# One encoder layer on one core: the in-projection in two passes, with the neighbourhood attention by bands of eight rows inside the second

## The chip, the core and the metric

The kernel is one program on one core of a Trainium2 chip. TensorE (PE) does the matrix products, and its weight loads (PEld) run beside them. VectorE (DVE), ScalarE (ACT) and GpSimd (POOL) do the elementwise work. SyncE (SP) issues the DMAs, in the order of the program. Each engine runs its own list of instructions in order and waits at semaphores for the others. The metric is the device time of one execution, in microseconds (us).

## What is computed

Two sequences of vectors of 1024 numbers go through one encoder layer with the same weights: a prompt of 512 tokens (s=0 in the code) and a sample of 2048 (s=1). Tokens stand in a grid of 64 columns, so the prompt has 8 rows and the sample 32. Cut to what matters:

```python
x = layer_norm(x, emb_ln_g, emb_ln_b)
z = x @ w_in                                   # 1024 -> 1952
qa, ka, va, fb, cq, ckv, kr, sg = split(z, [256, 256, 256, 256, 256, 128, 32, 512])
o_a = natten(qa, ka, va, na_rpb)               # 4 heads of 64
o_b = real(fft2(fb))                           # Fourier mix
o_c = mla(cq, ckv, kr, ...)                    # 4 heads, every query to every key
o_d = gating(gelu(sg), ...)                    # tokens mixed in chunks of 128
x = layer_norm(ALPHA * x + concat(o_a, o_b, o_c, o_d) @ w_out, ...)
x = layer_norm(ALPHA * x + conv_ffn(x), ...)   # 1024 -> 5632 -> 1024

def natten(q, k, v, rpb):      # row r, column c of the grid
    r0, c0 = clip(r - 4, 0, rows - 8), clip(c - 8, 0, 64 - 16)
    s = q[r, c] . k[r0:r0+8, c0:c0+16] / 8 + rpb[head, row offset, column offset]
    return softmax(s over the 128 neighbours) @ v[r0:r0+8, c0:c0+16]
```

All of it is float32. A product of float32 matrices is made of three products of a narrower type: each operand is split into a high part (a cast) and a low part (the rest), and `mm3` adds high x high, high x low and low x high.

## The kernel before

**Stages.** In `build` the stages stand one behind another: `phase1` (layer norm, in-projection, gating), `fourier` (the Fourier mix) with `mla_prep` (queries, keys and values of MLA) stepped inside it at every second of its yields, `natten` (neighbourhood attention) with what is left of `mla_prep`, then `mla`, `outproj` and the feed-forward part. `mla` is a generator; `natten` calls its first step, `next(ahead)`, twelve units before its own end.

**Order on the engines.** A scheduler places the instructions in each engine's list when the program is built. The code's order and the buffers of the pools (a tile waits until the buffer that it reuses is free) bind it, so an instruction can stand somewhat ahead of or behind its place in the code.

**phase1** goes over five blocks of 512 tokens, block 0 the prompt. All 14 weight tiles are loaded and split at the start (`load_w`, the high part on ScalarE, the low part L132 on GpSimd, or from the sixth tile on in turns on VectorE and GpSimd). For a block, `norm` loads four x tiles, normalises them on VectorE (L153, L162), applies the affine of the layer norm on GpSimd (L166, L167) and stores them; `turn` transposes them on TensorE (L350) and splits the result into the operands xTh and xTl. A block then takes 13 features (f, 128 outputs by 512 tokens, 24 products L139 to L141 each, ending on ScalarE at L364 or, for gelu, L368), the token products (L380 to L382, 288 columns each), and the gating (L409 and what goes before it). The norm of block b+1 stands behind feature 2, its turn behind the token products. `sgu_consts` loads the matrix of the gating and transposes it (L278) at the start, ahead of the features.

**natten** runs with whole sequences: for each sequence and pair of heads the query and key of all rows are loaded and split. A *unit* is eight rows of queries (a band) by 16 columns by one head, 128 queries on partitions. Its neighbours lie in a window of up to 16 rows by 32 columns, so the score product is 128 x 512 at most. For a unit:

- scores: three products on TensorE (`mm3`, L139 to L141, tile s);
- L683 on VectorE adds the table of biases and masks and takes the extreme value, L686 on ScalarE is the exponential with its sum, then a reciprocal on VectorE, and L689 scales, on GpSimd (VectorE for the prompt);
- flip: up to four transposes on TensorE (L705), split in the evacuation into ph and pl;
- values: products L724 and L725, for a group of four bands together, into one bank of 512 columns (o) that a product with zeros clears first (L719). A chunk of keys serves one or two bands, so these are 128 or 256 columns wide.

There are 16 prompt and 64 sample units, the prompt first. The flip of a unit is put three units behind its scores, with three banks for scores and five E buffers. The value windows are transposed by L643 (80 times 128 x 128), the tables added up by L666.

## Time and profile before

| | us |
|---|---|
| median of 3 runs | 3288.79 (3282.6 to 3290.15) |
| the profiled execution | 3299.96 |
| its span in the trace | 3298.2 |
| TensorE busy in the span | 3152.9 (96%) |
| VectorE busy | 2130.4 (65%) |
| ScalarE busy | 1390.7 (42%) |
| GpSimd busy | 1617.3 (49%) |
| start and in-projection | 0 to about 490 |
| Fourier mix with the MLA preparation | about 490 to 640 |
| neighbourhood attention | about 640 to 855 |
| MLA, out-projection, feed-forward | from about 855 |

The granted clock is the share of full speed that the chip allowed TensorE, 0.962 as a mean over this execution; 1.00 stands for 2.4 GHz, 0.50 for 1.2 GHz, and a value between them is a stretch with both. A busy time of TensorE counts what its products last at the clock that they had. A matmul's own duration contains its way through the array, so the pace of a row of products is read from the distance of their starts. The borders between stages are soft: the last work of one lies beside the first of the next.

### The profile page before, as it was taken

Reading aid. Unit: us, or ns where it says so; the run is one execution under the profiler, and the core shown is the slowest. Engines: PE = TensorE matmul, PEld = TensorE weight load, DVE = VectorE, ACT = ScalarE, POOL = GpSimd, SP = SyncE. Lnnn points to the kernel's source line nnn. Section 1 sums busy time; section 2 is a strip of 40 time slices with the busy share of each in tenths; the row PEclk is TensorE's granted clock in tenths of the full one; section 3 lists DMA queues with packets and bytes.
Section 4 is the critical chain, followed back from the end, with each engine's and each line's share of the span. In section 5 each row is a group of like instructions: output and inputs, shape, how many; then the busy total and the mean of one; then the engine's idle time right before and its main releaser. Section 6 shows DMA issues by size and latency. Waiting matters only on the chain.

```text
span 3298.2 us, 45978 instructions
## 1 busy us (share of the span) xinstructions
PE 3152.9 (96%) x16119; PEld 2739.0 (83%) x16119; DVE 2130.4 (65%) x3770; ACT 1390.7 (42%) x2493; POOL 1617.3 (49%) x1329
## 2 busy tenths in 40 slices
PE   7899999889999999998999999999899999999997
PEld 6788888767789998886899989999799997877785
DVE  6322216666888887445788866665567557679668
ACT  3221225545777677223544444433344323234224
POOL 6322313336666565234888856541354215466446
PEclk9999999867999999998999999999899999999998
DMA  7222144533210011545676769996599877547652
GB/s 222 87 88 72 71 122 129 172 105 103 91 38 22 22 41 48 161 144 170 226 251 234 244 218 346 335 313 211 183 349 336 276 244 256 216 168 284 227 209 103
DMA packets 369156, 588.35 MB, mean 178 GB/s; under 512 B 48409, under 2 KB 246905, under 8 KB 367389
## 3 DMA queue, kind: packets, MB, share of 16 engines
q1 hardware_dynamic: 368924, 585.41, 52.0%
q8 instruction: 128, 2.10, 0.3%
q14 instruction: 104, 0.84, 0.1%
HBM read 393.80 MB, written 191.51 MB: 177 GB/s over the span
## 4 chain that ended last, share of the span: by engine, by line
PE 84%; DVE 6%; DMA 5%; ACT 2%; issue 2%; SPq 1%; POOL 1%; DVEq 0%; ACTq 0%; POOLq 0%
PE s L1257 6%; PE s L1258 6%; PE s L1259 6%; PE t L1452 6%; PE t L1257 5%; PE t L1258 5%; PE t L1259 5%; PE s L139 4%; PE s L1452 4%; PE s L140 4%; PE s L141 4%; PE o L1452 4%; PE t L954 3%; PE mm L141 3%; PE mm L140 3%; PE mm L139 3%
## 5 line engine op out<-in xcount | busy, mean ns | idle before, releaser
L132 POOL TENSOR_TENSOR w<-wraw,w 128x512 fp32r<-128x512 f32 x162 | 235.5, 1459 | 315.1 <-ACT w L122 269.4
L1258 PE MATMUL s<-B,w 128*128 128x450 f32 (+1 forms) x792 | 285.4, 360 | 6.4 <-DVE B L132 6.4
L1257 PE MATMUL s<-B,w 128*128 128x450 f32 (+1 forms) x792 | 285.7, 363 | 0.6 <-ACT B L122 0.6
L1259 PE MATMUL s<-B,w 128*128 128x450 f32 (+1 forms) x792 | 284.9, 360 | 0.0
L1258 PE MATMUL t<-T,w 128*128 128x450 f32 (+1 forms) x792 | 283.8, 358 | 0.0
L1259 PE MATMUL t<-T,w 128*128 128x450 f32 (+1 forms) x792 | 283.7, 358 | 0.0
L1257 PE MATMUL t<-T,w 128*128 128x450 f32 (+1 forms) x792 | 282.1, 360 | 0.9 <-ACT T L122 0.9
L1265 DVE SCALAR_TENSOR_TENSOR h<-h,convc,h 128x896 f32<-128x896 f32 (+1 forms) x132 | 215.2, 1661 | 0.0
L926 DVE TENSOR_SCALAR_CACHE_REDUCE a<-s,low 128x512 f32<-128x512 f32 x272 | 195.0, 745 | 30.6 <-PE t L954 24.5
L140 PE MATMUL mm<-xTl,a 128*128 128x512 f32 x520 | 206.6, 397 | 2.2 <-DVE xTl L132 2.2
L141 PE MATMUL mm<-xTh,a 128*128 128x512 f32 x520 | 202.8, 393 | 0.0
L1264 DVE SCALAR_TENSOR_TENSOR h<-h,convc,h 128x896 f32<-128x896 f32 (+1 forms) x132 | 168.9, 1310 | 50.7 <-ACT h L1263 50.7
L139 PE MATMUL mm<-xTh,a 128*128 128x512 f32 x520 | 198.5, 395 | 1.4 <-ACT xTh L122 0.7
L1452 PE MATMUL t<-w,go 128*128 128x512 f32 x696 | 195.0, 399 | 4.9 <-ACT go L122 1.8
L1263 ACT ACTIVATE h<-h,convc 128x896 f32<-128x896 f32 (+1 forms) x132 | 138.3, 1096 | 133.3 <-DVE h L1138 130.8
L132 DVE TENSOR_TENSOR a<-t,a 128x512 fp32r<-128x512 f32 x240 | 161.1, 682 | 35.3 <-ACT a L122 34.7
L122 ACT CAST w<-wraw 128x512 fp32r<-128x512 f32 x166 | 102.1, 618 | 191.9 <-PE t L1259 132.7
L122 ACT CAST a<-t 128x512 fp32r<-128x512 f32 x240 | 134.4, 585 | 78.4 <-PE t L954 76.1
L1452 PEld LDWEIGHTS t<-w,go 128*128 128x128 f32 x696 | 131.1, 189 | 39.5 <-DVE x L1319 4.0
L1258 PEld LDWEIGHTS s<-B,w 128*128 128x128 f32 x792 | 150.7, 190 | 15.4 <-DVE B L132 6.7
L954 PE MATMUL t<-ident,a 128*128 128x128 f32 x1088 | 156.3, 274 | 6.1 <-DVE a L132 4.3
L122 ACT CAST go<-gs 128x256 fp32r<-128x256 f32 x200 | 78.2, 405 | 196.8 <-PE t L1452 65.2
(365 smaller groups left out, 9184.6 us busy)
## 6 DMA issues: line engine op xcount, KB each, us to landing
w<-wuops SPq DMA_DIRECT2D x220, 512.0 KB
wuops<-w SPq DMA_DIRECT2D x110, 512.0 KB
w<-wdops SPq DMA_DIRECT2D x104, 512.0 KB
wraw<-in_w_up_dram SPq DMA_DIRECT2D x88, 512.0 KB
wdops<-xs SPq DMA_DIRECT2D x74, 512.0 KB
graw<-g SPq DMA_DIRECT2D x100, 256.0 KB
wd<-wdops SPq DMA_DIRECT2D x48, 512.0 KB
g<-h SPq DMA_DIRECT2D x44, 448.0 KB
```

The costliest lines, as they stand in the source:

```text
L122: nc.scalar.copy(out, src)
L132: e.tensor_tensor(lo, src, hi.bitcast(F32), op=ALU.subtract)
L139: mm(ps, wh, xh, start=first, stop=False)
L140: mm(ps, wh, xl, start=False, stop=False)
L141: mm(ps, wl, xh, start=False, stop=last)
L926: nc.vector.tensor_scalar(e[:, c * 512:c * 512 + 512], ps, 1.0, self.low, op0=ALU.mult, op1=ALU.max, accum_out=m4[:, c:c + 1])
L954: nc.tensor.transpose(pt[:, k], e[:, kk * P:(kk + 1) * P], self.ident)
L1257: mm(ps[:, :hw], a, xh[:, k, :hw], start=first and k == 0, stop=False, skip_group_check=True)
L1258: mm(ps[:, :hw], a, xl[:, k, :hw], start=False, stop=False, skip_group_check=True)
L1259: mm(ps[:, :hw], b, xh[:, k, :hw], start=False, stop=last and k == KH - 1, skip_group_check=True)
L1265: nc.vector.scalar_tensor_tensor(c[:, :n], hb[:, 2:n + 2], cw[:, 2, ft:ft + 1], c[:, :n], op0=ALU.mult, op1=ALU.add)
L1452: mm = lambda a, b, st, sp_: nc.tensor.matmul(ps, a, b, start=st, stop=sp_, skip_group_check=True)
```

## The change

**The in-projection goes over the blocks twice.** The *near* pass makes features 0 to 7 of every block (query, key and value of the attention, and the Fourier input). Only eight weight tiles are loaded ahead of it; the others, the gating's constants and those of the convolution are loaded in blocks 1 and 2. The norm of block b+1 stands behind feature 0 of block b. Features 6 and 7 go as a pair, and after each of their eight steps one operand of the next block is transposed and split. The operands are also kept: 80 stores of 256 KB into `xd` in DRAM. The *far* pass makes features 8 to 12, the token products and the gating, with the operands loaded again by 20 loads of 1 MB.

**The attention runs inside the far pass.** It is a generator; `spent` counts the columns of projection products and steps it each time a sum of 92 is reached (54 for six products of a feature, 64 for a part of the token products). It goes by bands, the sample first: each band loads and splits its own queries and keys (`band`), each window its own values (`window`), and a unit's values go into a bank of their own, all products 128 columns wide, without the product of zeros. Tables are 512 wide at most, scalings and tables are on GpSimd throughout, there are three E buffers, two banks for scores and two for transposes, one for values, and the flip stands two units behind the scores.

**What moves for it.** `mla_prep` is stepped in three of four yields of `fourier` and finished there. The first step of `mla` stands behind `fourier`. Of the list of instructions, PE's grows from 15961 to 16185, ACT's from 2299 to 2411, with 57 loads of a function table in place of 17.

```diff
+NEAR = 8
+BANDS = ((("P", 0, 8),), (("A", 0, 12), ("B", 4, 16), ("B", 12, 16), ("C", 20, 12)))
+TICK = 92
...
                     for i, _ in enumerate(self.fourier(w2, s2)):
-                        if i % 2 == 0:
+                        if i % 4 < 3:
                             next(prep, None)
+                    for _ in prep:
+                        pass
                 with tc.tile_pool(name="mls", bufs=2, reuse_waits="tile") as ms:
                     mla = self.mla(ms)
-                    for _ in self.natten(mla, mps, s1):
-                        next(prep, None)
+                    next(mla)
...
-                self.split(raw[:, :, :n], wh[f][:, :, c0:c0 + n], wl[f][:, :, c0:c0 + n], "act", "dve" if i > 4 and i % 2 else "pool")
+                self.split(raw[:, :, :n], wh[f][:, :, c0:c0 + n], wl[f][:, :, c0:c0 + n], "act", "dve" if i > 4 else "pool")
...
+                def keep(b, k):
+                    for i in range(2):
+                        self.store(self.xd[b][:, k, i], xT[b][k][i].bitcast(F32))
...
+                def turn(b, k):
+                    ps, x = operand(b, k)
+                    self.evac(ps, x[0], x[1])
+                    keep(b, k)
...
+                extra = [lambda i=i: load_w(i) for i in range(NEAR, len(src_off))] + [sgu_consts, conv_consts]
+                norm(0)
+                turn0()
+                for b in range(nb):
+                    for f in range(NEAR - 2):
...
+                        if f == 0 and b + 1 < nb:
+                            norm(b + 1)
...
+                        if b and f and extra:
+                            extra.pop(0)()
+                    pair = [self.t(pp, [P, 512], "mm", bufs=4) for _ in range(2)]
+                    for k in range(KD):
+                        for i in range(2):
+                            step(pair[i], b, NEAR - 2 + i, k)
+                        if b + 1 < nb:
+                            turn(b + 1, k)
...
+                def spent(n):
+                    acc[0] += n
+                    while acc[0] >= TICK:
+                        acc[0] -= TICK
+                        next(nat, None)
...
+                def feat(b, f, uT):
+                    ps = self.t(pp, [P, 512], "mm", bufs=3)
+                    for k in range(KD):
+                        x = X[b][k]
+                        self.mm3(ps, wh[f][:, k], wl[f][:, k], x[:, 0], x[:, 1], k == 0, k == KD - 1)
+                        if k % 2:
+                            spent(54)
...
+            ps = self.t(pp, [P, 512], "s", bufs=2)
...
+            e = self.t(wp, [P, 512], "E", bufs=3)
...
+            po = self.t(pp, [P, P], "o", bufs=1)
+            for k in range(nck):
+                v = vr[:, k, hh].rearrange("p a d -> p (a d)")
+                nc.tensor.matmul(po, v, p[:, 0, k], start=k == 0, stop=False)
+                nc.tensor.matmul(po, v, p[:, 1, k], start=False, stop=k == nck - 1)
...
+        N, LAG = len(units), 2
...
+        for x in range(N + LAG + 1):
+            at(values, x - LAG - 1)
+            at(flip, x - LAG)
+            if x < N:
+                u = units[x]
+                if u[4] == 0:
+                    window(*u[:4])
+                scores(u)
+                if x + 2 < N:
+                    table(*units[x + 2])
+                if u[3:] == (2, 0) and x + 4 < N:
+                    band(*units[x + 4][:3])
+            yield
```

In the listings of instructions below a row is a line of the kernel, the operation, output<-inputs by tile and number, the size. The changed kernel's lines are a few higher: L142 to L144 are its `mm3`, L729 is its flip, L741 and L742 its values, L684 its window transposes, L169 and L170 its affine. First, GpSimd at the start, before: the affine of block 1 (tiles x_494 to x_500; x_165 is block 0's last) and the low parts of weights (a_.._..<-uv).

```order
L167 TENSOR_TENSOR x_165<-x_165,eb_140 128x1024
L132 TENSOR_TENSOR a_61_149<-uv_348,a_61_149 128x1024
L166 TENSOR_TENSOR x_494<-x_494,eg_139 128x1024
L132 TENSOR_TENSOR a_63_151<-uv_356,a_63_151 128x1024
L167 TENSOR_TENSOR x_494<-x_494,eb_140 128x1024
L166 TENSOR_TENSOR x_496<-x_496,eg_139 128x1024
L167 TENSOR_TENSOR x_496<-x_496,eb_140 128x1024
L166 TENSOR_TENSOR x_498<-x_498,eg_139 128x1024
L132 TENSOR_TENSOR a_65_153<-uv_364,a_65_153 128x1024
L166 TENSOR_TENSOR x_500<-x_500,eg_139 128x1024
L167 TENSOR_TENSOR x_498<-x_498,eb_140 128x1024
L167 TENSOR_TENSOR x_500<-x_500,eb_140 128x1024
```

The same place of the changed kernel (block 1 is x_397 to x_403).

```order
L170 TENSOR_TENSOR x_170<-x_170,eb_163 128x1024
L169 TENSOR_TENSOR x_397<-x_397,eg_162 128x1024
L170 TENSOR_TENSOR x_397<-x_397,eb_163 128x1024
L169 TENSOR_TENSOR x_399<-x_399,eg_162 128x1024
L170 TENSOR_TENSOR x_399<-x_399,eb_163 128x1024
L169 TENSOR_TENSOR x_401<-x_401,eg_162 128x1024
L169 TENSOR_TENSOR x_403<-x_403,eg_162 128x1024
L170 TENSOR_TENSOR x_401<-x_401,eb_163 128x1024
L170 TENSOR_TENSOR x_403<-x_403,eb_163 128x1024
```

The weights' low parts have left the rows of block 1's affine. Second, TensorE in the attention, before, some way into the sample: scores (s), flips (t<-flip), values (o).

```order
L139 MATMUL s_6253<-a_993_5557,a_991_5555 128x512
L140 MATMUL s_6253<-a_994_5558,a_991_5555 128x512
L141 MATMUL s_6253<-a_993_5557,a_992_5556 128x512
L705 MATMUL t_6163<-flip_65,E_6076 128x128 x3
L725 MATMUL o_6181<-pl_6106,a_1064_5777 128x128
L139 MATMUL s_6272<-a_993_5557,a_991_5555 128x512
L140 MATMUL s_6272<-a_994_5558,a_991_5555 128x512
L141 MATMUL s_6272<-a_993_5557,a_992_5556 128x512
L724 MATMUL o_6181<-ph_6105,a_1064_5777 128x256
L725 MATMUL o_6181<-pl_6106,a_1064_5777 128x256
```

After, in the far pass (mm are features of the projection; s_3203 are the scores of the unit whose E is E_3207):

```order
L142 MATMUL s_3203<-a_585_2816,q_2813 128x512
L143 MATMUL s_3203<-a_585_2816,q_2813 128x512
L144 MATMUL s_3203<-a_585_2816,q_2813 128x512
L143 MATMUL mm_3406<-a_420_2182,a_66_148 128x512
L729 MATMUL t_3032<-flip_65,E_2934 128x128 x4
L684 MATMUL t_3043<-ident_60,vw_3040 128x128 x4
L144 MATMUL mm_3406<-a_420_2182,a_66_148 128x512
L142 MATMUL mm_3406<-a_420_2182,a_66_148 128x512
```

About a hundred rows later on TensorE, where that unit's flip stands, behind the values of an older one:

```order
L741 MATMUL o_3231<-p_3190,vt_3042 128x128
L742 MATMUL o_3231<-p_3190,vt_3042 128x128
L729 MATMUL t_3288<-flip_65,E_3207 128x128 x4
L684 MATMUL t_3299<-ident_60,vw_3296 128x128 x4
L142 MATMUL s_3449<-a_585_2816,q_2813 128x512
L143 MATMUL s_3449<-a_585_2816,q_2813 128x512
L144 MATMUL s_3449<-a_585_2816,q_2813 128x512
L142 MATMUL mm_3624<-a_598_2898,a_68_150 128x512
```

Projection products and the work of older units now stand between a unit's scores and its flip; the values are pairs of 128 columns. Third, SP where MLA begins, before: loads of MLA's key pieces (raw<-K, raw<-Kr) among those of the attention (a_888<-z, mask, tbl).

```order
L117 DMA V_44_117<-vp_5167 128x4x256
L114 DMA mask_5236<-in_na_mask_dram 128x256
L114 DMA a_888_5271<-z_3_18_91 128x512
L114 DMA tbl_5238<-R_118 128x1x256
L114 DMA tbl_5268<-R_118 128x1x256
L117 DMA Kr_42_115<-q_5226 32x512
L114 DMA a_888_5271<-z_5_20_93 128x512
L114 DMA raw_7154<-Kr_42_115 32x512
L114 DMA raw_7160<-K_40_113 64x512
L114 DMA raw_7160<-Kr_42_115 32x512
L114 DMA raw_7165<-K_40_113 64x512
L114 DMA raw_7165<-Kr_42_115 32x512
```

After (mix<-ob are the last stores of the Fourier mix):

```order
L120 DMA Kr_42_115<-q_8149 32x512
L120 DMA mix_36_109<-ob_8179 128x4x128
L120 DMA mix_36_109<-ob_8231 128x4x128
L120 DMA mix_36_109<-ob_8283 128x4x128
L120 DMA mix_36_109<-ob_8335 128x4x128
L117 DMA raw_8343<-K_40_113 64x512
L117 DMA raw_8343<-Kr_42_115 32x512
L117 DMA raw_8349<-K_40_113 64x512
L117 DMA raw_8349<-Kr_42_115 32x512
L117 DMA raw_8354<-K_40_113 64x512
L117 DMA raw_8354<-Kr_42_115 32x512
L117 DMA wraw_11006<-in_w_out_dram 128x1024
```

The loads of MLA's keys have moved from among the attention's to behind the Fourier mix, and a load of w_out stands among them.

## Rows read from the trace of the kernel before

**Rows 1.** Busy time by stretch: from:to, length, busy of each engine, clock, DMA, GB/s.
```profile
core 0: us, PE busy (x) PEld busy (x) DVE busy (x) ACT busy (x) POOL busy (x), PEclk, DMA share, GB/s
110.00:490.00 380.00, 377.19 (x2030) 321.37 (x2029) 102.35 (x291) 77.38 (x155) 88.64 (x41) 1.00 0.25 85
...
690.00:820.00 130.00, 121.61 (x534) 93.91 (x534) 82.42 (x221) 73.79 (x182) 68.41 (x71) 0.71 0.34 98
900.00:1200.00 300.00, 299.57 (x2044) 270.13 (x2042) 253.93 (x696) 218.51 (x332) 194.21 (x172) 1.00 0.11 30
```

**Rows 2.** L380 of two blocks: durations in ns, first to last start, form.
```profile
L380 PE MATMUL mm<-w,xTh x32: 288/294/297, 110.4 to 122.7; 128*128 128x288 f32 x32
...
L380 PE MATMUL mm<-w,xTh x32: 288/294/297, 201.3 to 213.6; 128*128 128x288 f32 x32
```

**Rows 3.** Three lines around the attention, in the same view.
```profile
L571 ACT COPY q<-t x5: 569/572/577, 521.0 to 648.4; 32x512 f32<-32x512 f32 x5
...
L926 DVE TENSOR_SCALAR_CACHE_REDUCE a<-s,low x272: 730/747/753, 854.7 to 1312.6; 128x512 f32<-128x512 f32 x136
...
L725 PE MATMUL o<-pl,a x160: 273/364/581, 646.4 to 864.7; 128*128 128x256 f32 x96, 128*128 128x128 f32 x64
```

**Rows 4.** L683 by stretch: length, VectorE busy (entries), clock, DMA, GB/s.
```profile
690.00:820.00 130.00, 31.75 (x94) 0.71 0.34 98
820.00:850.00 30.00, 9.56 (x28) 0.99 0.18 48
```

**Rows 5.** TensorE in order of time: start, us, line, operation, form.
```profile
200.38 0.39 PE L141 MATMUL mm<-xTh,a 128*128 128x512 f32 x1
200.60 0.39 PE L139 MATMUL mm<-xTh,a 128*128 128x512 f32 x1
...
842.30 0.36 PE L725 MATMUL o<-pl,a 128*128 128x256 f32 x1
842.50 0.28 PE L724 MATMUL o<-ph,a 128*128 128x256 f32 x1
842.62 0.28 PE L725 MATMUL o<-pl,a 128*128 128x256 f32 x1
...
1004.28 1.04 PE L954 MATMUL t<-ident,a 128*128 128x128 f32 x8
1005.08 0.36 PE L971 MATMUL o<-a,a 128*128 128x256 f32 x1
```

**Rows 6.** Five microseconds of the start, columns as in rows 1.
```profile
90.00:95.00 5.00, 0.00 (x0) 0.00 (x0) 1.67 (x1) 1.37 (x4) 4.29 (x2) 0.50 0.30 100
```

**Rows 7.** What TensorE waited for until 110 us: total, times, longest.
```profile
PE tr L278 <- DMA uv<-in_sgu_w_dram: 8.2, 1, 8.2
```

**Rows 8.** GpSimd in order of time, the affine of block 1.
```profile
63.34 2.39 POOL L166 TENSOR_TENSOR x<-x,eg 128x1024 f32<-128x1024 f32 x1 [4.63 <-DVE x L162]
...
81.04 2.84 POOL L132 TENSOR_TENSOR a<-uv,a 128x1024 fp32r<-128x1024 f32 x1
...
87.17 4.63 POOL L167 TENSOR_TENSOR x<-x,eb 128x1024 f32<-128x1024 f32 x2
```

**Rows 9.** Block 2's normalisation in order of time, SP, VectorE and GpSimd.
```profile
140.72 1.79 SPq L114 DMA_DIRECT2D x<-in_x_sample_dram  x4
...
L153 DVE BATCH_NORM_STATS2 ln0st<-x x8: 673/676/695, 144.0 to 151.2; 128x6 f32<-128x512 f32 x8
...
153.03 8.10 POOL L166 TENSOR_TENSOR x<-x,eg 128x1024 f32<-128x1024 f32 x3 [17.60 <-PE mm L141]
...
165.79 7.10 POOL L167 TENSOR_TENSOR x<-x,eb 128x1024 f32<-128x1024 f32 x3
```

**Rows 10.** A group of instructions by line: count, busy and mean ns, idle before.
```profile
L132 DVE TENSOR_TENSOR a<-raw,a 96x512 fp32r<-96x512 f32 x5 | 7.6, 1550 | 0.7 <-ACT a L122 0.7
```

**Rows 11.** ScalarE in order of time, a load of a function table.
```profile
127.20 1.28 ACT L146 ACT_TABLE_LOAD   x1
128.50 0.31 ACT L146 ACTIVATE sgls<-sgmv,eps_ln 128x16 f32<-128x16 f32 x1
```

More of the change, by code (lines that the diff above doesn't have):

```diff
@@ L205, in build @@
             self.g = d([NF, P, sum(T for _, T in SEQS)], "g")
+            self.xd = [d([P, KD, 2, 512], f"xd{b}") for b in range(5)]
             self.wu = d([NF, 5, P, D], "wuops")
@@ L416, in phase1 @@
[L416 to L448 removed]
+                    for k in range(KD):
+                        keep(0, k)
@@ new lines, in phase1, with z_out @@
+            self.blocks = blocks
+            with pool("p1x") as xp, pool("p1p", space=bass.MemoryType.PSUM) as pp:
+                near(xp, pp)
+            with pool("p1n") as wp2, pool("p1q", space=bass.MemoryType.PSUM) as pp:
+                far(wp2, pp)
+    def z_out(self, sp, b, f, ps):
+        s, t0 = self.blocks[b]
+        zs = self.t(sp, [P, 512], "zs", bufs=3)
+        self.nc.scalar.activation(zs, ps, AF.Copy, scale=-0.125 if f in (2, 3) else 1.0)
+        dst = self.z[s][f] if f < 8 else self.c[s][f - 8]
+        self.store(dst[:, t0:t0 + 512], zs)
@@ L647, in prologue_v @@
[L647 to L653 removed]
+            vp = self.t(wp, [P, 4, 2, 2, 64], "vt", bufs=2)
+            vr = vp.bitcast(F32R)
+            ps = self.t(pp, [P, 4, 2, 64], "t", bufs=2)
+            for k in range(nch):
+                nc.tensor.transpose(ps[:, k].rearrange("p h d -> p (h d)"), vc[:, k * P:(k + 1) * P], self.ident)
+            nc.scalar.copy(vr[:, :nch, :, 0], ps[:, :nch])
@@ L661, in table @@
-            for ty in sorted(set(C["types"])):
-                off, n, ro = NA_TYPES[ty]
-                a0 = h * RSZ + (RO + ro) * 32 - 8 * ct
-                self.load(tbl[:, off - lo_c:off - lo_c + n],
-                          bass.AP(self.R.tensor, self.R.offset + a0, [[32, 8], [1, 16], [1, n]]))
-            (nc.gpsimd if s else nc.vector).tensor_tensor(tbl, tbl, st["mask"], op=ALU.add)
-            st["tbl", s, h, ct] = tbl
+                last["mask"] = self.t(wp, [P, 512], "mask")
@@ L783, in natten_body @@
             yield
-        for p in pend:
-            values(*p[1])
-        st["cm"].__exit__(None, None, None)
     def fourier(self, wp, sp):
```

615 lines of the change are left out of this document (265 added, 350 removed).

## The prediction

> **What bounds the kernel now.** I read the table by stage first [rows 1]. The in-projection (until 490 us) keeps TensorE busy for 377 of 380 us at the full granted clock, and a block of 512 tokens takes 90.9 us, from one block's token products (L380) to the next one's [rows 2]. The stretch from 490 to 640 is the Fourier mix with the MLA preparation. The neighbourhood attention fills 640 to 855: in its largest part TensorE is shown busy for 122 of 130 us, but at a granted clock of 0.71, a mix of the levels 1.2 and 2.4 GHz. MLA behind it runs at 1.00. So the attention stage is the one place before MLA where TensorE's work is paid at a worse price than its size, and this is where the change can gain. The stage ends where MLA's first scores are reduced, at 854.7; its own last value product L725 starts at 864.7, so some 12 us of it already lie beside MLA [rows 3].
>
> What a unit (one band, 16 columns, one head) costs there: L683 runs once a unit and shows two entries for it, so 94 entries are 47 units in 130 us, 2.77 us each, at clock 0.71; and 28 are 14 units in 30 us, 2.14 us each, at 0.99 [rows 4]. At the full clock a product of 512 columns follows the last after 0.226 us (200.38 to 200.60), one of 256 after 0.12 (842.50 to 842.62), the first of another kind about 0.08 later than that (842.30 to 842.50), and eight of 128 take 0.80 (1004.28 to 1005.08) [rows 5].
>
> **The change, term by term, against the profiled run** (3299.96 us, span 3298.2; the median of the runs shown is 3288.79, 0.34% lower, and the result is scaled by that).
>
> 1. The stage of its own goes: 640 to 855, minus 215 us, and the 12 us of it that lie beside MLA's start: minus 12.
>
> 2. Its TensorE work returns inside the second pass. By columns: scores are 98,304 columns, 192 times 512, at 0.226 us: 43 us; 256 flips and 128 window transposes at 0.10: 38 us; 512 value products of 128 columns at 0.10: 51 us. That is 133 us. (Before, values were 192 products of 256 columns, 128 of 128 and 16 of zeros, and the window transposes 80: bands cost 16 us more.) A unit changes the kind of product four times: 80 x 4 x 0.08 = 26. Sum 159 us. Lower end 133; upper end the pace of [rows 4] at the full clock, 64 x 2.14 + 16 x 1.07 (prompt units, half the columns) + 16 = 170. I take 159: the 2.14 us still holds waits that projection products can fill here.
>
> 3. Waits of TensorE in the second pass: plus 5 us (0 to 25). In the order of instructions, priced by [rows 5], the flips of a sample unit stand 9 to 22 us of TensorE work behind its scores, its value products mostly 4 to 10 us behind the flips. Between lie a reduction, an exponential, a reciprocal and a scaling, then an evacuation. All of a unit's work on VectorE is 82/47 = 1.75 us, on ScalarE 1.57, on GpSimd 1.46 [rows 1]: 4.8 us if nothing overlaps. 80 units load the three with 140, 126 and 117 us in a pass of some 370; with the pass's own work none exceeds 75%. What can still wait is an evacuation queued behind others, 1 us here and there.
>
> 4. The start. Before, block 0's token products begin at 110.4; its 13 features of 24 products are 70.5 us, so 40 us went to the start. TensorE has nothing from 90 to 95 [rows 6], since it waits 8.2 us for the load of sgu_w [rows 7]; that wait goes. But block 0's first pass is short (eight features of 5.42), and its last two features need block 1 normalised. On GpSimd the affine of block 1 starts at 63.3, waiting for VectorE, and ends at 91.8, with weight splits of 2.4 to 2.8 us between [rows 8]. The new order has none of them there, so I put the end at 80 (75 to 90). TensorE has done six features (32.5 us) at 60 to 65 and waits. Then the pair with the transposes takes 14 us, and 2 more at the lower clock: block 0's first pass ends at 96. Its work is 43.4 + 3.2 (32 transposes), so the start is 49 against 40: plus 9 us (-5 to +20).
>
> 5. Blocks 1 to 3 of the first pass: from the issue of the x loads at 140.7 to the end of the last affine at 172.9 are 32.2 us [rows 9]. Six features and a step of the pair give 33.9 us of cover. It fits by 2 us, and the stores of xd (16 of 256 KB a block) go ahead of the x loads. Plus 4 us (0 to 35).
>
> 6. Preparation and Fourier: the last preparation block stood partly beside attention, its last copy at 648.4 [rows 3]. Plus 3 us (0 to 9).
>
> 7. The end of the second pass: seven prompt units have their scores behind the last projection product, and nothing of the Fourier stage stands between them. Their own 8 us are in term 2; alone they run at their latency, some 2.5 us a unit: plus 10 us (5 to 15).
>
> 8. MLA's start. Before, K and Q of the first head were loaded and split beside attention. Now the K loads stand behind the last Fourier stores on SP's queue. A load lands 3.3 us after its issue (140.72 to the first statistics at 144.0) [rows 9]; four K chunks cost VectorE 1.55 us each [rows 10], then Q: about 12 us until the first scores. Then w_out's splits, moved here too, stand before the first scaling on GpSimd. Plus 12 us (5 to 20).
>
> The 80 stores of 256 KB and 20 loads of 1 MB of xd, 21 MB each way, I cost at nothing: the in-projection moved 85 GB/s at a DMA share of 0.25 [rows 1], so full engines would give 340 and 21 MB take 62 us of the pass's 370. Without that cover each 1 MB load would stop TensorE for about 3 us.
>
> Sum: -215 - 12 + 159 + 5 + 9 + 4 + 3 + 10 + 12 = -25 us: 3275 in the profiled run, 3264 in the median.
>
> **A rule against the change.** Gelu of the second pass and attention's exponential now alternate, and the instruction list holds 57 ACT_TABLE_LOADs instead of 17. In the trace one takes 1.28 us, from 127.20 to the next activation at 128.50 [rows 11], so 40 more are 51 us of ScalarE, off the path by term 3. The Trainium skill, "ScalarE: Activation LUTs", section "What ACT_TABLE_LOAD costs", adds a drain of about 1.38 us, 2.66 us a switch, and wants functions grouped by table set; by an estimate from that page 40 switches would take 106 us of ScalarE. The sum would still be -25, since ScalarE would stay under 85% of the pass.
>
> **Rivals.**
>
> A, slower: the first pass is bound by its chain of load, normalisation and affine. If the x loads queue behind a block's 4.2 MB of xd stores (13 us at full engines), the chain is 45 us against 33.9: 11 us for each of three blocks, and about 10 more for block 1. That is -25 + 33 + 10 = +18, or 3307 in the median. It decides from a chain of about 42 us. Against it: the stores issue while the pair of features runs, so most of them have gone when the x loads come.
>
> B, slower: ScalarE holds back the attention chain, each table load lying on the path: 40 x 1.28 = 51 us, +26, 3315. For it: ScalarE works in order, and a Gelu waits there for its feature's end. Against it: the 9 us of term 3.
>
> C, the change doesn't do what it says: units stop the products instead of hiding among them, since three E buffers and two score banks tie TensorE to the old pace. Then attention costs 64 x 2.77 + 16 x 1.39 = 199 us instead of 164, +10 in sum: 3299. The order of instructions, with its distances, speaks against it; the old pace of [rows 4], held with five E buffers, speaks for it.
>
> **How the numbers follow.** Forecast 0.70, A 0.13, B 0.05, C 0.12. The forecast's own spread is about 30 us either way, from bounds of which the largest are 37, 35 and 25 us wide: 3230 to 3295. What a measurement can tell from no change is about 0.2%, 6.6 us. Of the forecast's 0.70, 0.59 is faster, 0.08 the same and 0.03 slower; of A 0.11 is slower and 0.02, a milder form, the same; B is slower; C is 0.05 the same and 0.07 slower. Together: faster 0.59, same 0.15, slower 0.26. The range takes in A and most of C, and leaves B out: 3215 to 3312.
>
> **What would show it.** Terms 1 and 2: no attention beyond 20 us after the last projection product, and a granted clock of 1.00 throughout a second pass of some 370 us. Term 4: TensorE idle for 10 to 25 us before the first transposes of block 1. Term 5: idle before the transposes of later blocks under 3 us each; over 10 is rival A. Term 8: one gap of 10 to 15 us before MLA's first scores. Rival B would show TensorE's flips waiting, in the second pass, for what ScalarE released late; C a busy share under 90% there. The forecast is wrong if TensorE's busy share falls under 95% in the second pass, or if Fourier and preparation take over 165 us.

## The result, and the profile after

The changed kernel takes 3310.36 us (median of 4 runs, 3307.69 to 3312.97) against 3285.69 us: a ratio of 1.0074, interval 1.0057 to 1.0091. It is 25 us slower; the forecast was 3264. Its profiled run took 3309.91 us with a span of 3307.6. That of the kernel before (3299.96) lay 14 us above its median, so the profiled runs stand only 10 us apart; therefore the traces are compared by marks up to MLA's start, where the two kernels differ. All ratios here and below are to the kernel before, run on the same chip. The experiments stand on several chips, and between two of them a gain by medians and one by ratios differ by up to 4 us; the interval of a ratio is mostly 3 to 8 us either way.

The table by stage of the changed kernel answers to [rows 1] (from:to, length, busy time of each engine and instructions, granted clock, DMA share, GB/s).

```profile
281.00:500.00 219.00, 218.34 (x1280) 177.60 (x1279) 99.97 (x317) 129.19 (x263) 103.00 (x112) 1.00 0.51 156
...
600.00:620.00 20.00, 19.70 (x101) 15.96 (x100) 6.93 (x18) 4.40 (x12) 7.82 (x12) 0.61 0.25 73
...
680.00:700.00 20.00, 17.35 (x70) 14.42 (x70) 11.16 (x37) 9.33 (x30) 5.05 (x10) 0.50 0.08 28
...
720.00:740.00 20.00, 18.10 (x74) 16.14 (x73) 7.47 (x12) 10.82 (x18) 5.02 (x4) 0.66 0.58 196
```

The marks stand in the rows of single lines (durations in ns, first and last start, forms): the far pass's projection (L144), attention's values (L742), the last step of the Fourier mix (L144), MLA's first scores (L142). They answer to [rows 2, 3].

```profile
L144 PE MATMUL mm<-a,a x200: 387/389/504, 281.7 to 671.1; 128*128 128x512 f32 x100
...
L742 PE MATMUL o<-p,vt x256: 272/274/420, 309.2 to 699.8; 128*128 128x128 f32 x128
...
L144 PE MATMUL o<-Yh,l_dft x20: 387/398/628, 732.1 to 858.2; 128*128 128x512 f32 x20
...
L142 PE MATMUL s<-a,Q x272: 387/396/796, 870.7 to 1324.7; 96*128 96x512 f32 x136
```

The near pass ends at 281, the projection at 671, attention at 700, Fourier at 858. Then MLA's first transposes, after (L940) and, in a fence of its own, before (L954), with the end of the projection and of the Fourier mix before (L141):

```profile
L940 PE MATMUL t<-ident,a x1088: 270/272/421, 884.2 to 1339.8; 128*128 128x128 f32 x182
```

```profile
L954 PE MATMUL t<-ident,a x1088: 270/272/421, 867.6 to 1324.8; 128*128 128x128 f32 x182
...
L141 PE MATMUL mm<-xTh,a x14: 389/389/389, 479.8 to 488.6; 128*128 128x512 f32 x14
...
L141 PE MATMUL o<-Yh,l_dft x20: 387/393/398, 523.5 to 633.5; 128*128 128x512 f32 x20
```

884.2 against 867.6: 16.6 us late, where the sum of the prediction had them 25 us early, so 42 us are to be found. In the far pass TensorE is busy at full clock nearly throughout (386.7 of the 390 us until the last projection product, clock 0.98). What it waits for there and in the 29 us behind it is little (total, times, longest):

```profile
PE o L741 <- DVE oT L750: 3.8, 6, 1.0
PE t L729 <- DVE p L135: 2.1, 1, 2.1
PE t L729 <- POOL E L720: 1.9, 1, 1.9
PE mm L466 <- POOL uv L457: 0.3, 1, 0.3
```

Of these 8.1 us, 3.3 lie before the last projection product. So the attention does run beside the projection and hardly stops it, as the change says. The question is why that saves nothing.

### The profile page after: what moved, and what is told of

Same layout as the page of the kernel before. It is cut to its first block, busy times and chain, and to the rows that moved or that the text cites. A ratio compares the mean times of both kernels' runs of the same rounds, so it can differ in the third digit from the quotient of the medians.

```text
span 3307.6 us, 47204 instructions
## 1 busy us (share of the span) xinstructions
PE 3168.3 (96%) x16343; PEld 2747.4 (83%) x16343; DVE 2148.6 (65%) x3813; ACT 1467.5 (44%) x2605; POOL 1660.0 (50%) x1417
## 4 chain that ended last, share of the span: by engine, by line
PE 85%; DVE 4%; DMA 3%; issue 2%; POOL 2%; ACT 2%; SPq 1%; DVEq 0%; POOLq 0%; ACTq 0%
PE s L1243 6%; PE s L1244 6%; PE s L1245 6%; PE t L1438 6%; PE t L1243 5%; PE t L1244 5%; PE t L1245 5%; PE s L142 4%; PE s L1438 4%; PE s L143 4%; PE s L144 4%; PE t L940 3%; PE o L1438 3%; PE mm L142 3%; PE mm L144 3%; PE mm L143 3%
## 5 line engine op out<-in xcount | busy, mean ns | idle before, releaser
L928 POOL TENSOR_SCALAR a<-a,mrc 128x2048 f32<-128x2048 f32 (+1 forms) x80 | 138.5, 1734 | 45.1 <-DVE mrc L927 38.5
L925 ACT ACTIVATE a<-a,mnm,rq 128x2048 f32<-128x2048 f32 (+1 forms) x80 | 147.6, 1845 | 30.1 <-DVE mnm L923 30.0
L135 POOL TENSOR_TENSOR w<-s,w 128x512 fp32r<-128x512 f32 x84 | 142.2, 1704 | 34.7 <-ACT w L125 34.7
L1243 PEld LDWEIGHTS t<-T,w 128*128 128x128 f32 x792 | 149.7, 189 | 10.8 <-ACT T L125 1.5
```

Of the source, the lines that this page charges most:

```text
L135: e.tensor_tensor(lo, src, hi.bitcast(F32), op=ALU.subtract)
L1243: mm(ps[:, :hw], a, xh[:, k, :hw], start=first and k == 0, stop=False, skip_group_check=True)
```

## What attention costs in either kernel

Attention was left out of both kernels.

> The changed kernel with the attention left out (zeros are stored as its result); the two passes, the kept operands, the Fourier stage and MLA's start stay. Theory M (the prediction's term 2 was too small: attention's products cost TensorE some 183 us in the second pass, not 159, and the projection products between them some 15 us more than alone): the second pass falls from 419 us to about 222, so about 3113 us (3105 to 3120), and the pass shows products of 512 columns 0.226 us apart. Rival E (attention is as cheap as predicted, about 164 us, and the two passes themselves cost the rest): about 3146 us.

> The kernel before with the attention left out (zeros are stored); MLA's start is then no longer covered by attention, as in the changed kernel. Theory M: the stage of 215 us goes, about 15 us of MLA's start come into the open, so about 3086 us (3075 to 3096); against the changed kernel without attention the two passes alone then cost about 25 us, and attention costs about 200 us in either kernel. Rival E: attention costs 200 us here but 164 in the changed kernel, the two passes alone about 60.

In both, `natten` only stores zeros (here the changed kernel's; in the kernel before its first generator does the same, and MLA's first step follows).

```diff
     def natten(self, wp, pp):
+        o = self.t(wp, [P, 512], "oT", bufs=2)
+        self.nc.vector.memset(o, 0.0)
+        for s in (1, 0):
...
+                    self.store(self.mix[s][P * j:P * j + P, i * 512:(i + 1) * 512], o)
+        yield
```

Measured: 3114.76 us (ratio 0.948, 0.9459 to 0.9501) and 3100.96 us (0.9435, 0.9411 to 0.946). The first is theory M's number; the second is 5 us outside its range. Attention costs 3310 - 3115 = 196 us in the changed kernel and 3285 - 3101 = 184 in the one before. So of the 25 us 12 belong to attention, and 14 stand between the two kernels without it. Rival E falls. The old stage filled 215 us, but taking it away gives back only 184, since it covered other work. The rows of the kernel before without attention show what: the last Fourier product, MLA's first scores, and the wait between.

```profile
L141 PE MATMUL o<-Yh,l_dft x20: 387/393/628, 520.2 to 630.6; 128*128 128x512 f32 x20
...
L139 PE MATMUL s<-a,Q x26: 389/497/796, 659.9 to 697.7; 96*128 96x512 f32 x26
...
PE s L139 <- POOL Q L126: 25.8, 1, 25.8
```

The rest of the MLA preparation, the K and Q loads and their splits, 29 us from 630.6 to 659.9, lay beside attention before. And the two passes alone cost next to nothing up to the last projection product: without attention the changed kernel is there at 493 us, the kernel before at 491 (488.6 with attention). Of the 14 us between these two runs, 8 are there at MLA's first scores (668.3 against 659.9): the changed kernel has the rest of the preparation inside its Fourier stage.

```profile
L142 PE MATMUL mm<-xTh,a x320: 388/394/792, 19.4 to 276.7; 128*128 128x512 f32 x160
L142 PE MATMUL mm<-a,a x200: 387/389/499, 277.4 to 493.0; 128*128 128x512 f32 x100
```

In the profile, attention then takes the far pass from 216 us (277.4 to 493.6) to 419 (281.0 to 699.9): 203 us.

Is it hidden at all? The same units were put behind the far pass.

> The changed kernel with the attention by bands issued behind the second pass instead of inside it (one number, the step count between units). Theory M: TensorE's work of attention is the same 183 us; what the interleaving hides are only the waits of the chain and a lower clock, so 10 us more than the changed kernel (0 to 25): about 3320 us. Rival C (units stop the projection products in the second pass): the same or faster, 3295 to 3310. If the interleaving hid as much as predicted (about 50 us of the old stage), 3350 or more.

```diff
-TICK = 92
+TICK = 10 ** 9
```

Measured: 3385.05 us (its runs lie between 3360 and 3394), ratio 1.0289 (1.0243 to 1.0335), 75 us more than as changed: the last of the three readings, far above theory M's 10 us. The table by stage goes with it: the units alone keep TensorE busy for 263 of 270 us, at the lower of its two clocks from end to end.

```profile
510.00:780.00 270.00, 262.57 (x987) 213.35 (x985) 132.79 (x385) 126.58 (x328) 124.27 (x164) 0.50 0.34 91
```

So what the interleaving is worth goes with the clock (0.98 beside the projection), and rival C falls. What the units would take alone at the full clock, this run doesn't show. And the stage that was replaced, with whole sequences and wider value products, held 0.71 in its largest part and cost 184 us.

## Why the units cost 203 us and not 174: the row step

Start-to-start distances of TensorE's instructions from 281 to 700 us, added up by kind with waits left out, give 183 us for the attention's products (159 before the last projection product, 24 behind it at half the clock) and 228 for the projection's, which take 213 in the pass without attention. Term 2 had 159 for the attention's products and all changes of kind. Here is a unit's border in the changed kernel: the products in order of time, and the weight loads (PEld) of the same stretch (start, duration; in brackets the idle time before).

```profile
460.50 0.51 PE L729 MATMUL t<-flip,E 128*128 128x128 f32 x3
460.85 0.49 PE L684 MATMUL t<-ident,vw 128*128 128x128 f32 x3
461.27 0.45 PE L142 MATMUL s<-a,q 64*128 64x384 f32 x1
461.55 0.34 PE L143 MATMUL s<-a,q 64*128 64x384 f32 x1
461.73 0.34 PE L144 MATMUL s<-a,q 64*128 64x384 f32 x1
462.00 0.50 PE L143 MATMUL mm<-a,a 128*128 128x512 f32 x1
462.33 0.40 PE L144 MATMUL mm<-a,a 128*128 128x512 f32 x1
462.57 0.39 PE L142 MATMUL mm<-a,a 128*128 128x512 f32 x1
...
461.27 0.18 PEld L142 LDWEIGHTS s<-a,q 64*128 64x128 f32 x1 [0.17 <-issue]
...
462.00 0.19 PEld L143 LDWEIGHTS mm<-a,a 128*128 128x128 f32 x1 [0.25 <-issue]
```

The score products use 64 rows of the array (64*128), one head's channels; all else uses 128. At both steps, into 64 rows and out of them, the weight loads stand idle first (0.17 and 0.25 us), and the load starts only together with its product. The Trainium skill, "TensorE: Matmul & The Clock Gate", section "Step-by-step: what each phase is for", has a weight load pulled ahead of running products where the row groups don't conflict or the load goes to the background buffer; these rows agree with a pull that is lost at a change of rows, though why it is lost they don't show. It was tested by taking the step away.

> The changed kernel with scores over all 128 rows of query and key (the sum over two heads, so the heads are not kept apart); nothing else changes, the columns and the number of products are the same. Theory M1 (a change between products of 64 rows and of 128 rows is what costs TensorE time at a unit's borders, about 0.25 us a unit): 20 us less (10 to 26), about 3290 us, and the first score product is followed after the time of its columns. Rival M2 (any change of kind costs, whatever the rows): within 5 us of 3310.

```diff
-            kw = [k[:, x].rearrange("p (r c) -> p r c", c=GRID_W)[hs, :nr, CW[c]:CW[c] + 32] for x in range(2)]
-            self.mm3(ps[:, :n], q[hs, 0, c], q[hs, 1, c], kw[0], kw[1], True, True)
+            kw = [k[:, x].rearrange("p (r c) -> p r c", c=GRID_W)[:, :nr, CW[c]:CW[c] + 32] for x in range(2)]
+            self.mm3(ps[:, :n], q[:, 0, c], q[:, 1, c], kw[0], kw[1], True, True)
```

Measured: 3280.24 us, ratio 0.9984 (0.997 to 0.9999), 30 us less than as changed: M1, somewhat above its range. The same border, where no idle time stands before these two loads and they start ahead of their products (by 0.02 and 0.18 us):

```profile
446.59 0.51 PE L729 MATMUL t<-flip,E 128*128 128x128 f32 x3
446.94 0.49 PE L684 MATMUL t<-ident,vw 128*128 128x128 f32 x3
447.18 0.42 PE L142 MATMUL s<-a,q 128*128 128x384 f32 x1
447.44 0.34 PE L143 MATMUL s<-a,q 128*128 128x384 f32 x1
447.62 0.34 PE L144 MATMUL s<-a,q 128*128 128x384 f32 x1
447.80 0.40 PE L143 MATMUL mm<-a,a 128*128 128x512 f32 x1
448.04 0.40 PE L144 MATMUL mm<-a,a 128*128 128x512 f32 x1
448.27 0.40 PE L142 MATMUL mm<-a,a 128*128 128x512 f32 x1
...
447.16 0.19 PEld L142 LDWEIGHTS s<-a,q 128*128 128x128 f32 x1
...
447.62 0.19 PEld L143 LDWEIGHTS mm<-a,a 128*128 128x128 f32 x1
```

From the window's transposes to the third projection product behind are 1.72 us with the step (460.85 to 462.57) and 1.33 without (446.94 to 448.27): 0.39 us for this unit. Where scores follow a value or projection product instead of transposes, the step inwards costs 0.1 us and not 0.19, so the mean is some 0.34, or 27 us for 80 units. The sum of the distances falls from 183 to 156 us for attention (22 of them still behind the last projection product) and from 228 to 220 for the projection; part of the latter, an estimated 4 us, is that the clock fell less around 600 us (0.81 from 580 to 600 and 1.00 from 600 to 620). A version that keeps the heads apart holds the gain:

> The changed kernel with scores over 128 rows as in the run before, but with the heads kept apart: the query of a window is split into a tile for each head whose other 64 rows are zero. Six more small instructions a window on ScalarE and VectorE. Theory M1 (the step between 64 and 128 rows costs TensorE some 0.38 us a unit): 3282 us (3274 to 3292), against 3280 with heads not apart and 3310 as changed. If the small instructions on ScalarE and VectorE stand in the chain's way: 3295 or more.

```diff
+        qpads = [self.t(wp, [P, 2, 2, P], f"qp{x}", F32R) for x in range(3)]
+        for q in qpads:
+            nc.vector.memset(q.rearrange("p a b c -> p (a b c)").bitcast(F32), 0.0)
...
+            for hh in range(2):
+                hs = slice(64 * hh, 64 * hh + 64)
+                dh, dl = [q[hs, hh, x].rearrange("p (r q) -> p r q", q=16)[:, ::-1, ::-1] for x in range(2)]
+                self.split(src[hs], dh, dl, "act", "dve")
...
+            self.mm3(ps[:, :n], q[:, hh, 0], q[:, hh, 1], kw[0], kw[1], True, True)
```

Measured: 3279.67 us, ratio 0.9972 (0.9958 to 0.9987). But did the old stage pay the step too?

> The kernel before with scores over all 128 rows of query and key (the heads are not kept apart), as in the run of the changed kernel; columns and number of products are the same. Theory N (the old stage paid the step between 64 and 128 rows too, as often per unit): 20 to 30 us less, 3256 to 3268 us, so the step explains the size of the attention's price in both kernels, and not the difference between them. Rival (the old stage is bound by its chain and its clock, and TensorE's steps there cost nothing): 3278 to 3290; then the step is a price that the move into the second pass made visible.

```diff
-            self.mm3(ps[:, :n], qh[hs, i, c], ql[hs, i, c], ksl[0], ksl[1], True, True)
+            self.mm3(ps[:, :n], qh[:, i, c], ql[:, i, c], ksl[0], ksl[1], True, True)
```

(The key slices take all rows likewise.) Measured: 3266.08 us, ratio 0.9946 (0.9925 to 0.9966), 21 us less: theory N's number. But the clock changed with it. These rows answer to the one of 690 to 820 us in [rows 1] and to [rows 4] (L683):

```profile
690.00:820.00 130.00, 111.49 (x708) 98.24 (x708) 106.43 (x293) 93.24 (x231) 83.64 (x89) 0.95 0.38 110
...
790.00:820.00 30.00, 11.16 (x33) 1.00 0.23 67
```

From 690 to 820 us the clock is 0.95 instead of 0.71, with TensorE busy for less of the time (111 us for 122); what raised it isn't shown. At the full clock 33 entries are 16.5 units in 30 us, 1.82 us each, 0.32 less than the 2.14 of [rows 4]: about the step, in the old stage too. So the 21 us hold the step and a change of the clock, which the run doesn't separate. Of the 25 us between the kernels the step explains at most the difference of 30 and 21, which the intervals don't tell from nothing. (A version of the kernel before with zeros, heads apart, wasn't tried.)

## The tail: one bank for values

Seven units have their scores behind the last projection product, and from 671 to 700 us TensorE does their small work at a clock that falls to 0.50. First the units were issued more often.

> The changed kernel with a unit of attention every 84 columns instead of 92, so that all units but two or three have their scores before the last projection product. Theory (the seven units behind the second pass take 28 us for 8 us of work, and TensorE's clock falls there and stays low into the Fourier stage): 15 us less, 3295 us (3288 to 3303). Rival (denser units wait in the pass instead, since their chain is then the bound): 3306 to 3315.

```diff
-TICK = 92
+TICK = 84
```

Measured: 3306.06 us, ratio 1.0051 (1.0038 to 1.0063): 4 us less by the medians and 7 by the ratios, at the edge of the rival's range, with values until 694.5. In its trace there are still seven units' scores behind the last projection product. A unit's place is bound by its buffers too, and the tightest is the single bank of the value products, where TensorE also waits most (oT, 3.8 us above). So one bank was given over from the projection:

> The changed kernel with two banks for value products and two instead of three for the projection. In the order of instructions no unit's scores then stand behind the last projection product (seven before). Theory T (one value bank holds the units' pace down, and the tail of 28 us at half the clock is the price): the tail shrinks to under 8 us, about 20 us less, 3290 us (3283 to 3298). Rival (two banks for the projection make its products wait for evacuations, or the units only displace products): 3303 to 3315.

```diff
-            po = self.t(pp, [P, P], "o", bufs=1)
+            po = self.t(pp, [P, P], "o", bufs=2)
...
-                    ps = self.t(pp, [P, 512], "mm", bufs=3)
+                    ps = self.t(pp, [P, 512], "mm", bufs=2)
```

(And likewise for the other two tiles mm.) Measured: 3291.1 us, ratio 1.0018 (1.0009 to 1.0028), 19 us less: theory T. Attention now ends before the projection:

```profile
L144 PE MATMUL mm<-a,a x200: 387/392/506, 280.8 to 671.2; 128*128 128x512 f32 x100
...
L742 PE MATMUL o<-p,vt x256: 220/275/330, 308.3 to 664.2; 128*128 128x128 f32 x128
...
PE s L805 <- POOL h_dft L129: 9.4, 1, 9.4
```

The pass is no longer than before, though seven more units lie in it, since its clock is 1.00 from 600 to 620 us too; and behind it TensorE now waits 9.4 us for a table of the Fourier stage that GpSimd prepares (last row). So the 19 us are the tail's 29 and the dip in the pass, less the seven units' own work and this wait.

> The run before with scores over 128 rows, zeros in the other head's half, as well. If row step and tail add up: 3310 - 31 - 20 = 3259 us (3250 to 3268). If the row step was only cheap because the tail hid it, or the reverse: 3270 to 3280.

Measured: 3274.91 us, ratio 0.9965 (0.9954 to 0.9976). The two don't add up: with full rows the second bank gives only 5 us by the medians and 2 by the ratios, and the intervals overlap. In the profile the projection then ends at 658.7 us instead of 641.1: the seven units' products take 11 us more in the pass, TensorE waits 13 us in it instead of 8, and behind it stands the wait for the Fourier table again, 7.7 us.

## ScalarE's table loads, a wait on GpSimd, and the stages behind

> The changed kernel with gelu left out in the second pass (a copy in its place), so that 17 function tables are loaded instead of 57; everything else is as changed. Theory (ScalarE has the time): within 4 us of the changed kernel, 3306 to 3314. Rival B of the prediction (table loads stand on the path): 30 to 51 us less, 3260 to 3280.

```diff
-                        nc.scalar.activation(uT[:, f - 11], ps, AF.Gelu_apprx_tanh)
+                        nc.scalar.activation(uT[:, f - 11], ps, AF.Copy)
```

(And likewise for the token products.) Measured: 3299.01 us, ratio 1.0031 (1.0016 to 1.0045): 14 us less by the ratios (11 by the medians), between the two. Its trace has a clock of 1.00 from 600 to 620 us, where the changed kernel has 0.61, and its last projection product at 658.9 instead of 671.1. That points to what stands ahead of that stretch in the changed kernel, on GpSimd and TensorE:

```profile
594.91 2.38 POOL L456 TENSOR_TENSOR uv<-uv,sg 128x1024 f32<-128x1024 f32 x1
597.25 0.61 POOL L720 TENSOR_SCALAR E<-E,nar 128x384 f32<-128x384 f32 x1
...
597.91 0.55 PE L729 MATMUL t<-flip,E 128*128 128x128 f32 x3 [1.95 <-POOL E L720]
```

A unit's scaling (L720) stands behind the gating's affine (L456, 2.4 us); TensorE waits 1.95 us for it, and its granted clock falls behind that wait.

> The changed kernel with the gating's affine (two operations of 2.4 us a block on GpSimd) on VectorE. In the changed kernel a unit's scaling stands behind it on GpSimd at 595 us, TensorE waits 1.95 us and its granted clock is 0.61 in the 20 us behind. Theory (that one wait costs some 10 us through the clock): the granted clock is 1.00 from 600 to 620 and the run takes 8 us less, 3302 us (3298 to 3306). Rival (the clock falls for another reason, or elsewhere instead): 3307 to 3313.

```diff
-                    nc.gpsimd.tensor_tensor(v4, v4, bcast(sg, 4), op=ALU.mult)
-                    nc.gpsimd.tensor_tensor(v4, v4, bcast(sb, 4), op=ALU.add)
+                    nc.vector.tensor_tensor(v4, v4, bcast(sg, 4), op=ALU.mult)
+                    nc.vector.tensor_tensor(v4, v4, bcast(sb, 4), op=ALU.add)
```

Measured: 3303.2 us, ratio 1.0059 (1.0044 to 1.0074), in the theory's range. The clock is 1.00 there, and the last projection product again at 658.9, with all table loads in place:

```profile
600.00:620.00 20.00, 20.00 (x144) 18.15 (x143) 10.94 (x43) 11.63 (x28) 7.10 (x11) 1.00 0.25 75
```

So the 12 us in the pass go with that one wait and the clock behind it, which the run without gelu avoided by its other timing. By the ratios 5 us of them remain at the end, and the interval overlaps the changed kernel's, so the gain at the end isn't certain. What table loads as such cost is at most the 14 us of the run without gelu, and rather the 9 between these two runs, not the 51 of rival B; how much of the 9 it is stays open.

> The changed kernel with MLA's preparation stepped at every second yield of the Fourier stage, as before the change, and its last five steps behind the stage. Theory (that stage took 158 us against 142 because the preparation's remainder is now in it, whatever the cadence): within 5 us of 3310, since the remainder then stands in the open. Rival (three steps in four of products of one column starve TensorE and lower its clock at the stage's start): 8 to 15 us less, 3295 to 3302.

```diff
-                        if i % 4 < 3:
+                        if i % 2 == 0:
```

Measured: 3308.53 us, ratio 1.007 (1.0055 to 1.0085): the theory's time. The Fourier stage is shorter by 17 us (its last product at 841.1 instead of 858.2), and the wait for MLA's Q longer, 16.8 us instead of 11.9. MLA's first scores come 9 us earlier (861.4 for 870.7), its last ones only 5 (1320.0 for 1325.2). So what attention covered before stands in the open in either place, and most of the gain ahead of MLA is lost again in it.

> The changed kernel with the first MLA head's keys loaded and split, and its first query loaded, inside the Fourier stage (six of its steps before the end), as the attention stage covered them before; the raw tiles lie in arena slots that are free there. Theory (TensorE's 12 us of waiting ahead of MLA's first scores are the chain of loads behind the last Fourier stores): 10 us less, 3300 us (3297 to 3305). Rival (the wait is for something else, or is given back behind it): 3307 to 3313.

```diff
                     for i, _ in enumerate(self.fourier(w2, s2)):
                         if i % 4 < 3:
                             next(prep, None)
+                        if i == 43:
+                            for _ in prep:
+                                pass
+                            next(mla)
...
+            raw = first[0][:, c] if (s, h) == (1, 0) else self.t(sp, [P, 512], "raw", bufs=3)
```

Measured: 3305.84 us, ratio 1.0051 (1.0035 to 1.0066), 7 us less by the ratios and 5 by the medians, between the two ranges. The first scores come at 856.3 instead of 870.7, and 8.7 us go again to a wait for GpSimd's first scaling (L939):

```profile
PE t L951 <- POOL a L939: 8.7, 1, 8.7
```

## Parts together

> The changed kernel with four edits together: scores over 128 rows with zeros (heads apart), the first MLA keys inside the Fourier stage, the gating's affine on VectorE, and half of block 1's affine at the start on VectorE. If the parts add up: 3310 - 31 - 8 - 8 - 5 = 3258 us (3250 to 3270), which is below the kernel before. If their covers overlap: 3270 to 3280.

Measured: 3282.92 us, ratio 0.999 (0.9979 to 1.0): outside both ranges, and no faster than the rows with zeros alone (3279.67). The parts don't add up: the tail is 36 us there (projection until 635.0, values until 671.0; with the rows alone 641.1 and 672.7), so what the pass gains is lost behind it. With the second bank for values in place:

> As the run before, with the gating's affine and half of block 1's affine on VectorE. If these waits of 2 and 7 us count on top: 3250 us (3242 to 3258); if they are covered by then: within 4 us of the run before.

Measured: 3263.07 us, ratio 0.9925 (0.991 to 0.994): between the two expectations, 12 us below the run with rows and bank alone, and 23 below the kernel before, with the layer's result whole. The start's edit is this:

```diff
-                            self.affine(x, g_bc, b_bc)
+                            self.affine(x, g_bc, b_bc, "dve" if b == 1 and t % 2 else "pool")
```

> As the run before, with MLA's first keys loaded and split in the Fourier stage. Alone, that edit brought the first scores 14 us earlier, of which 9 were lost again ahead of the first transposes (w_out's splits stand before the first scaling on GpSimd). So 4 to 8 us less than the run before, some 3245 us; if it is lost again altogether, the same.

Measured: 3269.66 us, ratio 0.9947 (0.9929 to 0.9964): here the earlier keys cost 7 us instead of saving some, though MLA's first scores come 6 us earlier (817.6 for 823.8). Why isn't shown.

## Why the prediction was wrong

Term by term, in the profiled runs, for the 42 us between the sum and the mark:

- **Terms 2, 3 and 7 (attention in the far pass), 174 forecast, 203 measured.** The step that failed is the price in term 2 for a change of kind: its 0.08 us came from a value product behind flips, both on 128 rows [rows 5]. A unit's scores go through 64 rows and back, which costs some 0.34 us more in the mean. In the run with two banks all 80 units lie in the pass at a clock of 1.00, and there term 2 can be read: 162 us of attention's products and 15 more of the projection's (228 for 213) are 177, 18 above the forecast. With full rows as well, the same sum is 145 + 8 = 153, so between products of 128 rows the price was good enough. Term 7 was too low: 28.7 us from the last projection product to the last values, for 18 forecast, at a clock that falls to 0.50. Term 3 had few waits in the pass rightly (3.3 us for 5), but not what one of them does to the clock: 20 us at 0.61, an estimated 8 us. By these sums the three are 18 + 11 + 8, less the 5 of waits, which the pass without attention has as well: 32, for 29 by the marks.
- **The price stood in the trace before**, right behind the rows that were read for it: after three flips a value product starts 0.24 us later (842.06 to 842.30), after four a score product 0.53 later, where one flip more is 0.10.

```profile
842.06 0.49 PE L705 MATMUL t<-flip,E 128*128 128x128 f32 x3
842.30 0.36 PE L725 MATMUL o<-pl,a 128*128 128x256 f32 x1
...
842.86 0.60 PE L705 MATMUL t<-flip,E 128*128 128x128 f32 x4
843.39 0.44 PE L139 MATMUL s<-a,a 64*128 64x384 f32 x1
```

- **The pace of [rows 4].** Term 2's upper end was 170, from 2.14 us a unit, and 159 was taken because that pace was said to hold waits. With full rows the same pace is 1.82, so 0.32 of the 2.14 went with the scores on 64 rows: 20 us for 64 units, where 11 were taken off.
- **Term 1.** All 227 us of the old stage and its overlap were booked as gain, and 15 (terms 6 and 8) taken back for what it had covered: 212. Leaving the stage out gives 184 by the medians, and 197 from the profiled run that the terms refer to, which lay 14 us above its median. Where in the kernel those 14 us lie isn't shown.
- **Term 6, 3 forecast, 13.6 measured** (Fourier 488.8 to 633.5 before, 699.9 to 858.2 after). The remainder of the preparation that lay beside attention is five of its thirty steps, and a last copy at 648.4 [rows 3] doesn't show how much of it there was.
- **Term 8** had the wait right: 12 us forecast, 11.9 shown. From the last Fourier product to MLA's first transposes the sum left 19 us; it takes 26. Behind the wait 24 score products follow each other after some 0.43 us, until 881.6 (granted clock 0.50 from 870 to 882), and only then after 0.23, so by an estimate 5 of the 7 us are the lower clock.
- **Terms 4 and 5** came out 5 us too high: less the 203 of attention, the two passes take until 497, where the sum had 488.6 + 13. TensorE waits 13.3 us for block 1's affine, within the 10 to 25 forecast, the near pass ends at 281, and no wait for later blocks is shown between 110 and 285 us. Rival A's chain isn't there.

```profile
PE tr L324 <- POOL x L170: 13.3, 2, 10.9
...
PE s L142 <- POOL Q L129: 11.9, 1, 11.9
```

29 + 10.6 + 7 - 5 make the 42 us. No rival was the answer: A and C fell, and of B's 51 us at most 14 can be there. The slower outcome came from the forecast's own mechanism with its price too low and its gain too high. That 3310 us still lies in the range of 3215 to 3312 is luck: the range was stretched beyond the forecast's own 3230 to 3295 for A and C, and neither happened. C's price for attention, 199 us, is near the 203, but units didn't stop the products. Nor did either of the two signs of a wrong forecast show: TensorE was busy for 99% of the second pass until its last projection product, and Fourier and preparation took 158 us for the 165 named. What did show is the attention's end, 29 us behind the last projection product, where under 20 was expected, and the clock of 0.98 over 390 us in place of 1.00 over some 370.

The rule of the Trainium skill's "ScalarE: Activation LUTs", section "What ACT_TABLE_LOAD costs", isn't borne out in its drain: 51 loads of 1.28 us stand in the far pass with 1.0 us of idle time ahead of them in all, and no drain like the one stated there shows, before as after [rows 11].

## What to carry to other kernels

A stage is worth what the kernel loses without it, not its length: leave it out once and see what comes into the open (184 of 215 us here). Price interleaved products from pairs of the same shapes in the same order; here a step between 64 and 128 rows costs TensorE 0.1 to 0.2 us each way, and padding the short operand with zeros removes it, since the score products of 384 columns follow each other after 0.18 us on 64 rows as on 128. When work is woven into another loop, look at what its smallest buffer ring lets finish before that loop ends.

## What the runs showed of the hardware

At a unit's border the weight load of a product on 64 rows didn't start ahead of its product behind products on 128 rows, nor the reverse: 0.39 us for the pair of steps that is shown. And TensorE's clock: with 263 of 270 us shown busy by products of the attention alone, the granted clock was 0.50 throughout; beside the projection the same products had 0.98; one wait of 1.95 us amid them was followed by 20 us at a mean of 0.61. In the old attention stage the same number of score columns on 128 rows instead of 64 went with a clock of 0.95 instead of 0.71, in one trace of each.
